# A decoder layer on one core: low weight parts of the down projections formed by an accumulating DMA

## The chip, the core and the metric

The kernel runs on one core of a Trainium2 chip. The core has five engines with a queue each: TensorE (PE, with its weight loads shown as PEld), VectorE (DVE), ScalarE (ACT), GpSimd (POOL) and SyncE (SP), and 16 DMA engines that all queues share. Each queue works in order; the queues wait for each other by semaphores. The metric is the device time of one execution in microseconds (us), lower is better; a measurement here is the median of several executions.

## What is computed

One layer over 512 tokens of 1024 channels: a gated feed-forward block (FFN), a mixing stage (a gated linear recurrence beside a convolution), and a second FFN, each followed by a layer norm. The two FFNs are what the change touches:

```python
def swiglu(x, w_gate, w_up, w_down):
    return (jax.nn.silu(x @ w_gate) * (x @ w_up)) @ w_down

x = layer_norm(ALPHA * x + 0.5 * swiglu(x, ffn1_w_gate[l], ffn1_w_up[l], ffn1_w_down[l]), ...)
...
x = layer_norm(ALPHA * x + 0.5 * swiglu(x, ffn2_w_gate[l], ffn2_w_up[l], ffn2_w_down[l]), ...)
```

`w_gate` and `w_up` are 1024 x 2816, `w_down` is 2816 x 1024, all float32.

## The kernel before

**Products from two parts.** Every float32 operand is split into a high part `hi` (the value rounded to the type that TensorE multiplies, float32r) and a low part `lo` = value - `hi`, also float32r. Each product is three matmuls, hi x hi, hi x lo and lo x hi (`mm3`, lines 185 to 187, or line 400 for the gate and up products).

**Weights.** They are split on the fly. A *unit* is a 128 x 1024 tile of weights, 512 KB. `fetch` (line 80) loads it into one of two `raw` buffers by a DMA on SP's queue, ACT rounds it into `whi` (`cast`, line 66), and DVE, or for some weights POOL, subtracts `wlo` = `raw` - `whi` (`rest`, line 69). There are six pairs of `whi` and `wlo`; `ahead(n)` fetches units in the order of the list `todo` until n are ready or in the making, so up to four units beyond the one in use. The gate and up weights come as *quads* (1 MB in one `raw` buffer, which DVE also combines into sums); a quad takes three of the six pairs.

**A gate and up step.** For each pair f of 128-column blocks (0 to 10) and for s = 0 (gate) and s = 1 (up), seven products p1 to p7 run in the order p1, p7, p2, p4, p5, p6, p3 (a Strassen-like scheme that takes seven products where eight are usual). They accumulate in two PSUM tiles `a` and `b`, and some areas are used twice, with a copy by ACT (line 420) between:

```python
                ps = {"p1": a[:, 0], "p2": a[:, 0], "p6": a[:, 1],
                      "p7": b[:, 0], "p4": b[:, 0], "p5": b[:, 1], "p3": b[:, 1]}[n]
                yield from product(ps, x, w, n, n in ("p1", "p5", "p6", "p7"))
                if n in ("p1", "p7", "p5"):
                    nc.scalar.copy(work[:, {"p1": 0, "p7": 1, "p5": 2}[n]], ps)
```

p1, for example, must have been copied before p2 goes on accumulating in the same area, and only p7 lies between them. At the end of s = 0 the gate is put through SiLU by ACT (lines 484 and 485); the result `h[f]` is finished at the end of s = 1.

**The down projection.** `rows_out` multiplies h by `w_down` in two halves of 512 output columns, 11 units each, 22 units per FFN. A unit is used by 24 matmuls of 512 columns: four token tiles, two rows of 128, three matmuls. h itself is split into `hh`, `hl` (f = 0) and `hp` (f = 1 to 10) by ACT and DVE. In the second half the last four units are kept, and the token tiles are finished one after another, each followed by its layer norm (DVE, and `rstd` on POOL). The first units of the down projection are fetched while the last gate and up step runs; units are called u0 to u21 here.

**Who sets the order.** PE's order of work in these stages is as written (`manual_schedule`); on the other engines a scheduler orders instructions by its own estimates, within the dependences. A queue then runs in that order, whatever is ready.

Of the kernel before, what the change touches and what calls it, by code (L numbers as in the profile page):

```python
# [12 lines left out]
AF = mybir.ActivationFunctionType  # L13
ALU = mybir.AluOpType
# [9 lines left out]
NP = NF // 2  # L24
# [27 lines left out]
def decoder_layer(ctx, tc, x_tok, x_q, vec, bcast, ng, w_gu1, w_d1, w_i, w_g, w_col, w_o, w_gu2, w_d2, out):  # L52
    nc = tc.nc
# [11 lines left out]
    def cast(hi, raw):  # L65
        nc.scalar.copy(hi, raw)  # L66

    def rest(lo, raw, hi, engine=nc.vector):
        engine.tensor_tensor(lo, raw, hi.bitcast(F32), op=ALU.subtract)  # L69

    def split(raw, hi, lo, lo_engine):
        cast(hi, raw)
        rest(lo, raw, hi, lo_engine)
# [3 lines left out]
    def pair_of_parts():  # L77
        return (parts.tile([P, 1024], F32R, tag="whi", name="whi"), parts.tile([P, 1024], F32R, tag="wlo", name="wlo"))

    def fetch(src, shape, lo_engine):  # L80
        raw = raws.tile([P, 1024], F32, tag="raw", name="raw")
        hi, lo = pair_of_parts()
        nc.sync.dma_start(out=raw, in_=src)
        split(raw, hi, lo, lo_engine)
        a, b = shape
        return hi.rearrange("p (a b) -> p a b", a=a), lo.rearrange("p (a b) -> p a b", a=a)

# [58 lines left out]
    def ahead(n):  # L146

        while todo and sum(r[0] for r in ready) < n:
            what, *args = todo.popleft()
            if what == "unit":  # L150
                ready.append([1, fetch(*args)])
            else:
                q = Quad(*args)
                q.load(0, 4)
                getattr(q, what)()
                ready.append([3 if what == "seven" else 2, q.of])

    def plan(srcs, shape, lo_engine):
        todo.extend(("unit", s, shape, lo_engine) for s in srcs)

    def plan_quads(src, first):
        todo.extend(("plain" if f < PLAIN else "seven", src[f, s]) for f in range(first, NP) for s in range(2))
# [7 lines left out]

    tok, ch = (2, 512), (NK, P)
    plan_quads(w_gu1, 1)
    plan([w_d1[h, u] for h in range(2) for u in range(NP)], tok, nc.vector)
    plan([w_col[n] for n in (8, 9, 10, 11)], ch, nc.vector)
    plan([w_col[n] for n in (0, 4, 1, 5, 12, 13, 14, 15)], ch, nc.gpsimd)
    plan([w_i[u] for u in range(4)], tok, nc.gpsimd)
# [2 lines left out]
    plan([w_o[0, u] for u in (2, 3)], tok, nc.gpsimd)  # L179
    plan([w_o[0, u] for u in (0, 1)] + [w_o[1, u] for u in (2, 3, 0, 1)], tok, nc.vector)  # L180
    plan_quads(w_gu2, 0)
    plan([w_d2[h, u] for h in range(2) for u in range(NP)], tok, nc.vector)

    def mm3(ps, lh, ll, rh, rl, first, last):
        nc.tensor.matmul(ps, lhsT=lh, rhs=rh, start=first, stop=False)  # L185
# [375 lines left out]
    with tc.tile_pool(name="first", bufs=1) as fst:  # L561
# [9 lines left out]
        for half, a, b in ((0, 0, 1), (0, 1, 2), (0, 2, 4), (1, 0, 2), (1, 2, 4)):  # L571
            raw = x1.raw[half][:, a:b]
# [414 lines left out]
```

## Time and profile before

| | |
|---|---|
| median of 3 runs | 954.01 us (952.9 to 954.87) |
| the profiled execution | 953.89 us, of which the span from the first to the last instruction is 952.2 us |
| PE busy | 932.9 us, 98% of the span |
| DVE, ACT, POOL busy | 699.0, 380.0, 121.7 us |
| first FFN, gate and up | about 7 to 235 us |
| first FFN, down | about 235 to 345 us |
| mixing stage | about 345 to 604 us |
| second FFN, gate and up, then down | about 604 to 824 us, 824 to 944 us |

The span is what the trace covers; the 1.7 us beside it lie outside the first and last instruction. An engine's busy time says what it did, not what it held up: that is read from the waits.

### The profile page before, as it was taken

How to read it: one execution, taken by the hardware profiler on the slowest of the kernel's cores; microseconds unless marked ns; L12 is line 12 of the kernel's file. 1: busy time of each engine (PE TensorE's matmuls, PEld its weight loads, DVE VectorE, ACT ScalarE, POOL GpSimd, SP SyncE). 2: the span in 40 equal slices, each digit the busy share in tenths (PEclk: the TensorE clock that was granted, in tenths of full speed). 3: DMA queues.
4: the chain of work that ended last, by engine and by line, in shares of the span. 5: the costliest groups of instructions: out<-in, count | busy, mean ns of one | idle time of the engine just before them, and what ended most of it. 6: DMA issues, size and time to landing. Idle time of an engine off the chain costs nothing.

```text
span 952.2 us, 14214 instructions
## 1 busy us (share of the span) xinstructions
PE 932.9 (98%) x5904; PEld 844.3 (89%) x5904; DVE 699.0 (73%) x923; ACT 380.0 (40%) x545; POOL 121.7 (13%) x107
## 2 busy tenths in 40 slices
PE   7999999999999999999999999999999999999996
PEld 6899999999888889887888878989999999988885
DVE  7978888887724275999897657958888888742417
ACT  5555555555421123313331723535555555722100
POOL 9100000000000035522352103200000000000002
PEclk9999999999999999999999999999999999999998
DMA  8432332324422303412130141222323322452202
GB/s 279 180 119 89 106 116 89 129 72 144 146 98 89 110 23 114 130 46 64 51 122 8 52 170 45 89 89 96 127 90 116 107 89 80 130 167 89 92 20 88
DMA packets 23200, 96.67 MB, mean 102 GB/s; under 512 B 2448, under 2 KB 5008, under 8 KB 17760
## 3 DMA queue, kind: packets, MB, share of 16 engines
q1 hardware_dynamic: 23024, 95.43, 29.7%
q8 instruction: 46, 0.75, 0.3%
q0 software_dynamic: 112, 0.34, 0.1%
q14 instruction: 18, 0.15, 0.1%
HBM read 93.66 MB, written 2.10 MB: 101 GB/s over the span
## 4 chain that ended last, share of the span: by engine, by line
PE 81%; DVE 10%; issue 3%; POOL 2%; DMA 1%; ACT 1%; POOLq 0%; DVEq 0%; ACTq 0%
PE bank L400 38%; PE bank L186 13%; PE bank L187 13%; PE bank L185 13%; DVE bank L745 4%; PE bank L762 2%; POOL wlo L69 1%; DMA raw<-w_col 1%; DVE wlo L69 1%; DVE m L794 1%; POOL rstd L213 1%; DVE fq L712 1%; DVE diag L802 1%; DVE xres L338 0%; DVE totals L798 0%
## 5 line engine op out<-in xcount | busy, mean ns | idle before, releaser
L69 DVE TENSOR_TENSOR wlo<-raw,whi 128x1024 fp32r<-128x1024 f32 (+2 forms) x148 | 176.9, 1201 | 147.8 <-ACT whi L66 147.7
L66 ACT CAST whi<-raw 128x1024 fp32r<-128x1024 f32 (+2 forms) x170 | 173.0, 1022 | 261.0 <-PE bank L187 149.7
L185 PE MATMUL bank<-whi,hp 128*128 128x512 f32 x320 | 124.7, 390 | 0.0
L187 PE MATMUL bank<-whi,hp 128*128 128x512 f32 x320 | 124.5, 389 | 0.0
L186 PE MATMUL bank<-wlo,hp 128*128 128x512 f32 x320 | 124.5, 389 | 0.0
L400 PE MATMUL bank<-bh,whi 128*128 128x256 f32 x432 | 122.3, 283 | 0.0
L400 PE MATMUL bank<-bl,whi 128*128 128x256 f32 x432 | 122.3, 283 | 0.0
L400 PE MATMUL bank<-ah,whi 128*128 128x256 f32 x432 | 122.2, 283 | 0.0
L400 PE MATMUL bank<-ah,wlo 128*128 128x256 f32 x432 | 122.2, 283 | 0.0
L400 PE MATMUL bank<-al,whi 128*128 128x256 f32 x432 | 122.2, 283 | 0.0
L400 PE MATMUL bank<-bh,wlo 128*128 128x256 f32 x432 | 122.1, 283 | 0.0
L400 PEld LDWEIGHTS bank<-bh,whi 128*128 128x128 f32 x432 | 82.9, 192 | 0.0
L400 PEld LDWEIGHTS bank<-bl,whi 128*128 128x128 f32 x432 | 82.9, 192 | 0.0
L400 PEld LDWEIGHTS bank<-bh,wlo 128*128 128x128 f32 x432 | 82.9, 192 | 0.0
L400 PEld LDWEIGHTS bank<-al,whi 128*128 128x128 f32 x432 | 82.8, 192 | 0.1
L400 PEld LDWEIGHTS bank<-ah,whi 128*128 128x128 f32 x432 | 82.8, 192 | 0.1
L400 PEld LDWEIGHTS bank<-ah,wlo 128*128 128x128 f32 x432 | 82.8, 192 | 0.0
L745 DVE SCALAR_TENSOR_TENSOR bank<-u,vecs,bank 128x512 f32<-128x512 f32 x120 | 82.1, 747 | 0.2
L212 POOL TENSOR_SCALAR rstd<-mv 128x1 f32<-128x1 f32 x16 | 8.1, 506 | 501.1 <-DVE mv L330 485.9
L187 PEld LDWEIGHTS bank<-whi,hp 128*128 128x128 f32 x320 | 60.1, 188 | 12.6
L185 PEld LDWEIGHTS bank<-whi,hp 128*128 128x128 f32 x320 | 60.1, 188 | 12.4
L186 PEld LDWEIGHTS bank<-wlo,hp 128*128 128x128 f32 x320 | 60.1, 188 | 12.2
(191 smaller groups left out, 1950.8 us busy)
## 6 DMA issues: line engine op xcount, KB each, us to landing
raw<-w_gu SPq DMA_DIRECT2D x42, 1024.0 KB, 4.8
raw<-w_d SPq DMA_DIRECT2D x44, 512.0 KB, 3.5
raw<-w_col SPq DMA_DIRECT2D x16, 512.0 KB, 3.5
raw<-w_o SPq DMA_DIRECT2D x8, 512.0 KB, 3.6
xres<-x_tok SPq DMA_DIRECT2D x4, 512.0 KB, 7.8
gb<-bcast SPq DMA_DIRECT2D x4, 512.0 KB, 4.3
raw<-w_i SPq DMA_DIRECT2D x4, 512.0 KB, 3.5
raw<-w_g SPq DMA_DIRECT2D x4, 512.0 KB, 3.5
```

Of the source, the lines that this page charges most:

```text
L66: nc.scalar.copy(hi, raw)
L69: engine.tensor_tensor(lo, raw, hi.bitcast(F32), op=ALU.subtract)
L185: nc.tensor.matmul(ps, lhsT=lh, rhs=rh, start=first, stop=False)
L186: nc.tensor.matmul(ps, lhsT=lh, rhs=rl, start=False, stop=False)
L187: nc.tensor.matmul(ps, lhsT=ll, rhs=rh, start=False, stop=last)
L213: nc.gpsimd.tensor_tensor(r, r, negh.broadcast_to([P, n]) if n > 1 else negh, op=ALU.pow)
L400: nc.tensor.matmul(ps, lhsT=l[:, k, :], rhs=r[:, k, :], start=first and k == 0 and j == 0, stop=k == 3 and j == 2, skip_group_check=True)
L712: nc.vector.tensor_scalar(f, s, oml[:, h:h + 1], lb[:, h:h + 1], op0=ALU.mult, op1=ALU.add)
L745: nc.vector.scalar_tensor_tensor(accs[n], us[n][:, j:j + T], vecs[:, w:w + 1], accs[n], op0=ALU.mult, op1=ALU.add)
L762: nc.tensor.matmul(ps[:, g, :], lhsT=k[:, h, sl], rhs=q[:, h, sl], start=True, stop=True)
L794: nc.vector.tensor_tensor(ov, ov, tv, op=ALU.mult)
L802: nc.vector.copy_predicated(diag[h], masks[:, n:n + 1, :].broadcast_to([P, NT, P]), ps)
```

## The change

For the 44 units of the two down projections DVE no longer subtracts. ACT makes two passes over `raw`: it rounds it into `whi` as before, and writes -`raw`, rounded to the same type, into `wlo`, which is -`whi`. Then a DMA on POOL's queue reads the same weights from memory a second time and adds them to `wlo`, so that `wlo` ends as `raw` - `whi`. A DMA that adds to its destination is issued on POOL's queue.

```diff
         nc.sync.dma_start(out=raw, in_=src)
-        split(raw, hi, lo, lo_engine)
+        if lo_engine is None:
+
+            cast(hi, raw)
+            nc.scalar.activation(lo, raw, AF.Copy, scale=-1.0)
+            nc.gpsimd.dma_start(out=lo, in_=src, accum_op=ALU.add)
+        else:
+            split(raw, hi, lo, lo_engine)
...
-    plan([w_d1[h, u] for h in range(2) for u in range(NP)], tok, nc.vector)
+    plan([w_d1[h, u] for h in range(2) for u in range(NP)], tok, None)
...
-    plan([w_d2[h, u] for h in range(2) for u in range(NP)], tok, nc.vector)
+    plan([w_d2[h, u] for h in range(2) for u in range(NP)], tok, None)
```

Lines behind the change move by six: lines 420, 484 and 485 are 426, 490 and 491 afterwards. The negation is line 87, the accumulating DMA line 88.

The change also moves instructions on the queues. On ACT, at the last gate and up pair (f = 10) of either FFN, the queue before reads as follows, from the copies of p1 and p7 of s = 0 (into `h`) over the casts of u0, u1 and u2 to the SiLU and the copy of p1 of s = 1 (into `work`):

```order
L420 COPY h<-bank_2370 128x256
L420 COPY h<-bank_2371 128x256
L66 CAST whi<-raw 128x1024 x2
L420 COPY h<-bank_2371 128x256
L66 CAST whi<-raw 128x1024
L484 ACTIVATE h<-bank_2370 128x256
L485 ACTIVATE h<-h 128x768
L420 COPY work<-bank_2484 128x256
L66 CAST hh<-h 128x1024
L420 COPY work<-bank_2485 128x256
```

And the same place of ACT's queue after the change:

```order
L426 COPY h<-bank_2370 128x256
L426 COPY h<-bank_2371 128x256
L66 CAST whi<-raw 128x1024
L87 ACTIVATE wlo<-raw 128x1024
L66 CAST whi<-raw 128x1024
L426 COPY h<-bank_2371 128x256
L87 ACTIVATE wlo<-raw 128x1024
L66 CAST whi<-raw 128x1024
L87 ACTIVATE wlo<-raw 128x1024
L490 ACTIVATE h<-bank_2370 128x256
L491 ACTIVATE h<-h 128x768
L426 COPY work<-bank_2487 128x256
```

The negation of u0 stands right behind its cast, that of u1 behind the copy of p5, and that of u2 between its cast and the SiLU, so ahead of the copy of p1 as well.

On POOL, from the scaling of the residual early in the first FFN to the first norm, the queue before holds only the clearing of two mixing buffers (`diag`) and one load (`ngb`):

```order
L288 TENSOR_SCALAR xres_76<-xres_76 128x1024
L667 MEMSET diag_3641 128x512
L665 DMA ngb<-ng 128x512
L667 MEMSET diag_3642 128x512
L212 TENSOR_SCALAR rstd<-mv 128x1
```

After the change the 22 accumulating DMAs of the first FFN stand there too:

```order
L294 TENSOR_SCALAR xres_76<-xres_76 128x1024
L88 DMA wlo<-w_d 128x1024 x2
L671 DMA ngb<-ng 128x512
L88 DMA wlo<-w_d 128x1024
L673 MEMSET diag_3663 128x512
L88 DMA wlo<-w_d 128x1024 x2
L673 MEMSET diag_3664 128x512
L88 DMA wlo<-w_d 128x1024 x17
L218 TENSOR_SCALAR rstd<-mv 128x1
```

The first five are interleaved with the load and the two clearings, and all 22 stand ahead of the norms; in the second FFN the other 22 stand in one piece ahead of the norms. PE's order is the same before and after.

## Rows read from the trace of the kernel before

**Rows 1.** Page, busy time of each engine, share, instructions.

```profile
PE 932.9 (98%) x5904; PEld 844.3 (89%) x5904; DVE 699.0 (73%) x923; ACT 380.0 (40%) x545; POOL 121.7 (13%) x107
```

**Rows 2.** Windows: us, busy by engine (instructions), granted clock, DMA share, GB/s.

```profile
52.00:235.80 183.80, 183.80 (x1516) 182.66 (x1515) 155.29 (x209) 96.78 (x145) 1.34 (x3) 1.00 0.31 105
235.80:300.00 64.20, 64.20 (x285) 53.16 (x284) 32.38 (x34) 20.41 (x21) 0.25 (x1) 1.00 0.36 116
...
824.00:890.00 66.00, 66.00 (x294) 54.71 (x293) 33.04 (x36) 21.30 (x22) 0.00 (x0) 1.00 0.36 117
```

**Rows 3.** Waits of PE, longest first: total us, times, longest.

```profile
PE bank L185 <- ACT whi L66: 5.1, 1, 5.1
PE bank L279 <- DVE xres L338: 1.2, 1, 1.2
```

**Rows 4.** Groups by line and shape: busy us, mean ns, idle before.

```profile
L69 DVE TENSOR_TENSOR wlo<-raw,whi 128x1024 fp32r<-128x1024 f32 x138 | 169.6, 1233 | 147.8 <-ACT whi L66 147.7
L66 ACT CAST whi<-raw 128x1024 fp32r<-128x1024 f32 x160 | 168.0, 1053 | 260.2 <-PE bank L187 149.7 <-PE bank L186 38.4 <-PE bank L400 30.9
```

**Rows 5.** Timeline of ACT, first FFN: start, duration, instruction, idle before.

```profile
219.45 1.05 ACT L66 CAST whi<-raw 128x1024 fp32r<-128x1024 f32 x1 [0.94 <-PE bank L400]
...
225.40 1.05 ACT L66 CAST whi<-raw 128x1024 fp32r<-128x1024 f32 x1 [1.75 <-PE bank L400]
226.59 0.39 ACT L484 ACTIVATE h<-bank 128x256 f32<-128x256 f32 x1
226.87 0.84 ACT L485 ACTIVATE h<-h 128x768 f32<-128x768 f32 x1
227.61 0.36 ACT L420 COPY work<-bank 128x256 f32<-128x256 f32 x1
```

**Rows 6.** Timelines of DVE and SP at the same place.

```profile
220.53 1.23 DVE L69 TENSOR_TENSOR wlo<-raw,whi 128x1024 fp32r<-128x1024 f32 x1 [1.45 <-ACT whi L66]
...
225.87 0.69 DVE L431 TENSOR_TENSOR h<-bank,h 128x512 f32<-128x512 f32 x1
...
221.78 0.33 SPq L83 DMA_DIRECT2D raw<-w_d  x1
```

**Rows 7.** Timeline of PE at the start of p2.

```profile
227.99 0.28 PE L400 MATMUL bank<-bh,wlo 128*128 128x256 f32 x1
228.11 0.30 PE L400 MATMUL bank<-ah,whi 128*128 128x256 f32 x1
```

**Rows 8.** Timelines of ACT and PE, the same place of the second FFN.

```profile
814.19 1.05 ACT L66 CAST whi<-raw 128x1024 fp32r<-128x1024 f32 x1 [1.69 <-DMA raw<-w_d]
815.45 0.39 ACT L484 ACTIVATE h<-bank 128x256 f32<-128x256 f32 x1 [0.21 <-DVE h L431]
...
816.46 0.36 ACT L420 COPY work<-bank 128x256 f32<-128x256 f32 x1
...
816.96 0.30 PE L400 MATMUL bank<-ah,whi 128*128 128x256 f32 x1
```

**Rows 9.** Timelines of ACT and PE in the first down projection.

```profile
251.96 1.06 ACT L66 CAST whi<-raw 128x1024 fp32r<-128x1024 f32 x1 [2.48 <-PE bank L187]
...
322.68 1.05 ACT L66 CAST whi<-raw 128x1024 fp32r<-128x1024 f32 x1 [4.38 <-PE bank L187]
...
235.65 0.40 PE L186 MATMUL bank<-wlo,hh 128*128 128x512 f32 x1
...
337.67 0.39 PE L186 MATMUL bank<-wlo,hp 128*128 128x512 f32 x1
```

**Rows 10.** Page, DMA issues: instructions, KB each, us from issue to landing.

```profile
raw<-w_gu SPq DMA_DIRECT2D x42, 1024.0 KB, 4.8
raw<-w_d SPq DMA_DIRECT2D x44, 512.0 KB, 3.5
...
xres<-x_tok SPq DMA_DIRECT2D x4, 512.0 KB, 7.8
```

**Rows 11.** Windows: four units of the down projection's steady part.

```profile
262.84:284.60 21.76, 21.76 (x97) 18.02 (x96) 4.90 (x4) 4.22 (x4) 0.00 (x0) 1.00 0.30 97
```

**Rows 12.** Timeline of POOL before the down projection.

```profile
225.80 0.60 POOL L665 DMA_DIRECT2D ngb<-ng  x1
235.52 0.53 POOL L667 MEMSET diag<- 128x512 f32 x1 [9.12 <-PE bank L400]
```

## The prediction

> **What bounds the kernel now.** I read the busy times first, then the windows by stage, then PE's waits, and last the timelines at the place where the waits nearly touch. PE is busy for 932.9 of 952.2 us [rows 1]. That is an average; the windows say where the rest lies. From 52 us to the end of the first down projection, and in the second down projection, PE's busy time equals the window: 183.80 of 183.80, 64.20 of 64.20, 66.00 of 66.00, at full granted clock [rows 2]. The list of PE's waits holds nothing of a down projection: the longest is 5.1 us in the first products of the program, the next 1.2 us at a norm [rows 3]. So in the stages that the change touches, PE alone sets the time, and there is no wait that a faster VectorE could end. What is to be found out is whether the new way of making `wlo` is late somewhere.
>
> **What is removed: nothing on the path.** 44 subtractions by DVE of 1.233 us [rows 4] are 54.3 us. PE never stood waiting for them, so they are worth 0. DVE's later work in the mixing stage is not reached by it, since the order changes only around the down projections. I find no gain to book.
>
> **What is added, in the steady part: hidden.** Each unit gets a second ACT pass, which I price like the cast beside it, 1.05 us [rows 4]; the widest other ACT row, 0.84 us for 768 columns [rows 5], would scale to 1.12 us. Back to back a pass takes about 0.1 us less (226.87 to 227.61 is 0.74 us for an instruction of 0.84 us [rows 5]), so 0.95 us. Then comes a DMA on POOL's queue. The casts of u8 and u21 are 70.72 us apart, 13 steps of 5.44 us [rows 9]; that is PE's time for a unit, and ACT sits idle for 4.38 us of each. ACT's queue has room. The tightest units are the ends. u0 is cast at 219.45 and negated by 221.45, and its `wlo` is first used at 235.65: 14.2 us are left for the DMA [rows 5, 9]. u21 is cast at 322.68, negated by 324.7, used at 337.67: 13.0 us [rows 9]. The trace has no accumulating transfer. From below it is at least a plain load of the same bytes, 3.5 us to landing; from above the slowest 512 KB of the trace, the loads of `xres`, took 7.8 us; I take 4.8 us, the row for 1024 KB, since 512 KB of weights and 512 KB of `wlo` are read [rows 10]. Either end is below 13.0 us. Without that cover every us beyond it would be a us of PE.
>
> POOL's queue is in order: a DMA that waits for its negation holds up what stands behind it. That is the `ngb` load, the two clearings of `diag` (both wanted only in the mixing stage) and, behind u21's DMA, the norms, which begin after 337.67 us, when POOL is long free. The other way round, the second clearing waits for PE until 235.52 [rows 12] and stands ahead of u5's DMA; u5 is used at 235.65 + 5 x 5.44 = 262.9, so that costs nothing.
>
> **What is added at the end of gate and up: a stall in either FFN.** Here ACT is not free to be late. In the step f = 10, s = 1, ACT must copy p1 out of PSUM before p2 accumulates there. Before the change it copies from 227.61 to 227.97 and PE starts p2 at 228.11, 0.12 us after the matmul before it, its normal pitch [rows 5, 7]. So PE waits for nothing, and has at most 0.1 us to spare (0.05 taken). Ahead of this copy in ACT's queue stand SiLU (two instructions) and u2's cast; now u2's negation comes between the cast and SiLU. Step by step, in us:
> - `raw` of u2 uses the buffer of u0. SP issues it at 221.78, as DVE's subtraction of u0 ends at 221.76 [rows 6]; the cast of u2 follows at 225.40 [rows 5]. Now the buffer comes free with u0's negation, at 219.45 + 0.95 + 1.05 = 221.45, so 0.31 earlier. But the accumulating DMA of u0 is released by that same negation and shares the DMA engines with the load. Call what this costs the load c.
> - u2: cast at 225.09 + c, negation at 226.04 + c, SiLU at 226.99 + c. SiLU was at 226.59, held by DVE's step that ended at 226.56 [rows 5, 6]. It and the copy of p1 come 0.40 + c later, and p2 0.35 + c.
> - In the second FFN the cast is at 814.19, SiLU 1.26 later and p2 at 816.96, 0.14 behind the copy's end [rows 8]: -0.31 + c + 1.90 - 1.26 = 0.33 + c, less the 0.05 to spare 0.28 + c.
>
> The two stalls sum to 0.63 + 2c. PE has no idle time behind them to take it back: all later work starts that much later.
>
> **c.** From below 0: the load may have moved its bytes before the other begins. From above 7.8 - 3.5 = 4.3 [rows 10]. A load that shares with another 512 KB should behave like one of 1024 KB, 4.8 - 3.5 = 1.3; POOL takes 0.60 to issue where SP takes 0.33 [rows 6, 12], so the other starts some 0.3 later: I take c = 1.0. Sum: 0.63 + 2.0 = 2.6 us on the profiled execution's 953.89, which is 0.12 below the median: 956.5 us, 0.3% slower. The bounds of c give 954.5 and 963.1.
>
> That row stands for a single queue, the two transfers here are on two. The Trainium skill (DMA: Bandwidth & Descriptors, Issuing engines are not separate DMA queues) says that DMAs from SP, ACT and GpSimd run on the same 16 engines and interleave. By that rule c is the whole 1.3 and the sum 3.2 us; with queues that did not touch each other it would be 0.6 us. No row here has two queues at work at once, so the trace neither bears it out nor speaks against it.
>
> **Rivals.**
> - *No measurable change.* c is small, because POOL's DMA starts to move bytes when the load has nearly landed. The deciding point is 0.63 + 2c = 1.9 us, so c = 0.64. For it: POOL's later start. Against: both are released at the same moment, and the load then has 3.5 us to go. At c = 0.1 the time is 954.7 us. 0.2%, 1.9 us, is about what a measurement of this kernel can tell from no change.
> - *The accumulating DMA is the bound.* In the steady part four plain loads keep all DMA engines busy for 0.30 of 21.76 us [rows 11], 1.63 us each. Between u0's negation at 221.45 and u21's use at 337.67 lie 116.2 us, in which 22 accumulating transfers, 20 loads and two gain and bias loads must fit: 22a + 36 = 116 gives a = 3.65, so 2.2 times a plain load. At two loads' worth (3.26) it fits. At three (4.9) each stage ends 27.7 us late: 1009 us. If they ran one after another at 7.8 us, 22 x 7.8 - 116.2 = 55.4 us per stage: 1065 us. For it: nothing in the trace bounds a transfer that adds. Against: the reads are only doubled. The Trainium skill (Collectives: The Full Stack, The bandwidth ceiling) says that a reduction is half as fast as a copy because of its second source read and not because of the add; by that rule a is 3.26 and this rival costs nothing. No run here shows it.
> - *Faster.* DVE, relieved of its `wlo` work, finishes the last sums of the gate earlier (SiLU waited for it [rows 8]) and ACT gains what the negation costs. That takes a negation behind the copy, which the queue's order rules out: the most it could give is the 0.2 us of that wait in either FFN, 953.5 us.
>
> **How the numbers follow.** The stall of 1.9 to 9 us in all: 0.56. No measurable change: 0.26. DMA as the bound: 0.14, all slower. Faster by over 0.2%: 0.04, kept for a mechanism that I do not see. So slower is 0.70, same 0.26, faster 0.04. The range leaves out the third case and the fourth: from 953.6, just under c = 0, to 962.0, c near 4.
>
> **What would show it.** PE's waits should get a new row, line 406 for ACT's copy at line 426, twice, some 1 to 2 us each, just ahead of the down projections, and on ACT's timeline u2's cast, negation, SiLU and copy should stand in one chain without idle time. The load of u2's `raw` should land 4 to 5 us after its issue. The windows of the down projections should stay full of PE. Wrong would be: waits of PE at line 192 for a DMA of `wlo` (then the second rival), or no new wait at all with c near 0 (the first). DMA share in the steady part should rise from 0.30 to 0.6 to 0.9.

## The result: 0.97% slower, by waits at the end of gate and up that the prediction had only half of

The changed kernel takes 962.22 us (961.7 to 965.97, 4 runs) where the kernel before takes 953.45 us in the same comparison (952.81 to 954.87, 4 runs): a ratio of 1.0097, 95% interval 1.0082 to 1.0113. The forecast was 956.5 us, with a range up to 962.0. The profiled execution is the slowest of the four, 965.97 us with a span of 964.3; the parts below are of its own 12.1 us of span over the one before, not of the median's 8.8.

The page's busy times and queues, to be set beside [rows 1]:

```profile
PE 938.3 (97%) x5904; PEld 848.4 (88%) x5904; DVE 646.2 (67%) x879; ACT 420.6 (44%) x589; POOL 161.7 (17%) x151
...
q1 hardware_dynamic: 23024, 95.43, 29.3%
q0 software_dynamic: 6448, 23.41, 14.2%
...
raw<-w_d SPq DMA_DIRECT2D x44, 512.0 KB, 6.6
wlo<-w_d POOLq DMA_DIRECT2D x44, 512.0 KB, 7.3
```

The change did what it says. DVE's busy time fell by 52.8 us, ACT's rose by 40.6 us, and POOL's queue (q0, the software one) moved 23.41 MB. The loads of the down projection's weights, untouched by the diff, now take 6.6 us to land where they took 3.5 [rows 10].

PE's waits, longest first; the first row has no counterpart in [rows 3]:

```profile
PE bank L406 <- ACT work L426: 6.9, 4, 2.9
PE bank L191 <- ACT whi L66: 5.0, 1, 5.0
```

There are four such waits, two in either FFN; in the same list no wait at line 192 is for a DMA, and that is where `wlo` is used. The windows say where the time goes (us, then busy time and instructions of PE, PEld, DVE, ACT, POOL, then granted clock, DMA share, GB/s):

```profile
52.00:222.00 170.00, 170.00 (x1403) 169.00 (x1402) 145.37 (x195) 88.44 (x133) 0.00 (x0) 1.00 0.29 100
222.00:232.00 10.00, 9.37 (x77) 9.12 (x77) 3.10 (x5) 6.77 (x10) 3.76 (x5) 1.00 0.93 220
232.00:236.00 4.00, 3.22 (x27) 3.02 (x26) 0.00 (x0) 2.00 (x2) 0.53 (x1) 1.00 1.04 275
236.00:242.00 6.00, 4.12 (x16) 3.83 (x17) 2.58 (x6) 4.37 (x6) 1.69 (x3) 0.60 0.98 225
242.00:248.00 6.00, 6.00 (x24) 4.85 (x23) 6.00 (x6) 4.78 (x6) 0.85 (x1) 0.84 0.95 217
...
262.00:346.00 84.00, 84.00 (x372) 69.57 (x371) 8.04 (x11) 28.07 (x28) 11.02 (x13) 1.00 0.86 200
```

Up to 222 us and from 262 us PE is as full as before. In between it idles, and its granted clock falls to 0.60 and 0.84 over two windows. The DMA engines are busy all through the change's part, already at 0.93 in the ten us in which gate and up still runs.

How a wait comes about is seen on ACT's timeline at that place (start, duration, instruction, idle before and what ended it), the counterpart of [rows 5]:

```profile
225.88 1.05 ACT L66 CAST whi<-raw 128x1024 fp32r<-128x1024 f32 x1 [0.97 <-DMA raw<-w_d]
226.84 1.05 ACT L87 ACTIVATE wlo<-raw 128x1024 fp32r<-128x1024 f32 x1
227.79 0.36 ACT L490 ACTIVATE h<-bank 128x256 f32<-128x256 f32 x1
228.06 0.83 ACT L491 ACTIVATE h<-h 128x768 f32<-128x768 f32 x1
228.79 0.36 ACT L426 COPY work<-bank 128x256 f32<-128x256 f32 x1
...
233.17 1.05 ACT L66 CAST whi<-raw 128x1024 fp32r<-128x1024 f32 x1 [2.80 <-DMA raw<-w_d]
234.12 1.05 ACT L87 ACTIVATE wlo<-raw 128x1024 fp32r<-128x1024 f32 x1
236.51 1.04 ACT L66 CAST whi<-raw 128x1024 fp32r<-128x1024 f32 x1 [1.33 <-DMA raw<-w_d]
237.46 0.36 ACT L426 COPY work<-bank 128x256 f32<-128x256 f32 x1
```

And PE's timeline, the last product before and the first after either wait, then the first down products:

```profile
228.30 0.28 PE L406 MATMUL bank<-bh,wlo 128*128 128x256 f32 x1
229.20 0.39 PE L406 MATMUL bank<-ah,whi 128*128 128x256 f32 x1 [0.63 <-ACT work L426]
...
234.94 0.28 PE L406 MATMUL bank<-bh,wlo 128*128 128x256 f32 x1
237.88 0.58 PE L406 MATMUL bank<-ah,w2hi 128*128 128x256 f32 x1 [2.65 <-ACT work L426]
238.26 0.41 PE L406 MATMUL bank<-al,w2hi 128*128 128x256 f32 x1
238.47 0.41 PE L406 MATMUL bank<-ah,w2lo 128*128 128x256 f32 x1
...
241.03 0.63 PE L192 MATMUL bank<-wlo,hh 128*128 128x512 f32 x1
241.46 0.63 PE L193 MATMUL bank<-whi,hl 128*128 128x512 f32 x1
```

First read the copy at 228.79: u2's cast, negation, SiLU and this copy stand in one chain without idle time, and p2 starts right behind it, as forecast. Then read the copy at 237.46. It is that of p5, which must be out of PSUM before p3; it stands behind u4's cast, and that cast waited until 236.5 for its load. SP issued this load at 227.9:

```profile
227.91 0.33 SPq L83 DMA_DIRECT2D raw<-w_d  x1
```

So a load that takes 3.5 us when alone [rows 10] took 8.5 us. On the chain of work that ended last it is the longest single step of that stretch:

```profile
227.91 8.52 DMA raw<-w_d
```

In the kernel before, p5's copy stood behind u4's cast too, and the cast was on time:

```profile
232.51 1.05 ACT L66 CAST whi<-raw 128x1024 fp32r<-128x1024 f32 x1 [1.83 <-PE bank L400]
233.47 0.37 ACT L420 COPY work<-bank 128x256 f32<-128x256 f32 x1
...
233.89 0.38 PE L400 MATMUL bank<-ah,w2hi 128*128 128x256 f32 x1
```

That copy ended at 233.84 and p3 began right behind it, at 233.89, so there was no room behind the cast. Ahead of it there was some: u4's load landed 1.0 us before the cast, which PE held up. Of the 4.7 us by which the load takes longer now (8.5 against 3.8 at this place before), this 1.0 us and the 0.8 us by which PE itself is late since p2 are covered; PE waits for about the rest.

The loss of the profiled execution, from matmul to matmul with the normal pitch of 0.12 us taken off, is 0.78 us at p2 and 2.82 us at p3 in the first FFN, and by the same reading 0.90 and 3.04 us in the second, 7.5 us of waiting. The last of these waits, between the matmuls before and after it:

```profile
829.94 0.28 PE L406 MATMUL bank<-bh,wlo 128*128 128x256 f32 x1
833.10 0.39 PE L406 MATMUL bank<-ah,w2hi 128*128 128x256 f32 x1 [2.88 <-ACT work L426]
```

After the waits at p3 matmuls come at about half pace, in the first FFN at once, in the second after ten matmuls at full pace (1.3 us): 0.21 us apart where 0.12 is usual, and 0.43 where 0.23 is usual for 512 columns. That is the lower of the clock's two levels, 1.2 GHz instead of 2.4 (granted clock 0.50 from 238.3 to 243.5 us). It lasts for 12 matmuls of p3 and about 8 of the longer ones in the first FFN (12 x 0.094 + 8 x 0.2 = 2.7 us) and about 8 of the longer ones in the second (1.6 us). Together with the waits that is 11.8 of the 12.1 us.

The clock's part differs from execution to execution. The mean granted clock was 0.993 here and 0.996, 0.996 and 0.998 in the other three, where the executions of the kernel before have 0.995 to 0.999. The one at 0.998 took 962.60 us, so a loss of some 9 us arises also where the clock shows no loss. How much of the median's 8.8 us the clock makes stays open, as only the slowest of the four was profiled.

### The profile page after: what moved, and what is told of

It is laid out like the page before. It is cut to its first block, busy times and chain, and to the rows that moved or that the text cites. A ratio compares the mean times of both kernels' runs of the same rounds, so it can differ in the third digit from the quotient of the medians.

```text
span 964.3 us, 14287 instructions
## 1 busy us (share of the span) xinstructions
PE 938.3 (97%) x5904; PEld 848.4 (88%) x5904; DVE 646.2 (67%) x879; ACT 420.6 (44%) x589; POOL 161.7 (17%) x151
## 3 DMA queue, kind: packets, MB, share of 16 engines
q0 software_dynamic: 6448, 23.41, 14.2%
## 4 chain that ended last, share of the span: by engine, by line
PE 77%; DVE 11%; issue 4%; DMA 3%; ACT 2%; POOL 2%; POOLq 0%; DVEq 0%; ACTq 0%
PE bank L406 35%; PE bank L192 13%; PE bank L193 13%; PE bank L191 13%; DVE bank L751 4%; DMA raw<-w_d 3%; PE bank L768 2%; DVE xres L344 1%; POOL wlo L69 1%; DVE wlo L69 1%; ACT whi L66 1%; DVE m L800 1%; POOL rstd L219 1%; DVE fq L718 1%; DVE diag L808 1%
## 5 line engine op out<-in xcount | busy, mean ns | idle before, releaser
L69 DVE TENSOR_TENSOR wlo<-raw,whi 128x1024 fp32r<-128x1024 f32 (+2 forms) x104 | 123.2, 1193 | 66.9 <-ACT whi L66 66.9
L88 POOL DMA_DIRECT2D wlo<-w_d x44 | 38.0, 863 | 572.1 <-ACT wlo L87 551.0
L330 DVE SCALAR_TENSOR_TENSOR xres<-bank,xres 128x512 f32<-128x512 f32 x24 | 16.4, 687 | 131.3 <-PE bank L193 131.3
L87 ACT ACTIVATE wlo<-raw 128x1024 fp32r<-128x1024 f32 x44 | 46.6, 1059 | 93.6 <-PE bank L192 68.7
L193 PEld LDWEIGHTS bank<-whi,hp 128*128 128x128 f32 x320 | 60.1, 188 | 12.6
```

What stands on the lines that cost most here:

```text
L87: nc.scalar.activation(lo, raw, AF.Copy, scale=-1.0)
L88: nc.gpsimd.dma_start(out=lo, in_=src, accum_op=ALU.add)
L193: nc.tensor.matmul(ps, lhsT=ll, rhs=rh, start=False, stop=last)
L330: nc.vector.scalar_tensor_tensor(z, acc[i], factor, z, op0=ALU.mult, op1=ALU.add)
```

## The experiments

Two theories were set against each other, and a third beside them. **Late loads**: the accumulating DMAs crowd the loads of u2 to u4; the casts of these units wait in ACT's queue ahead of the copies of p1 and p5, and PE waits for the copies. **A longer ACT queue**: the second passes delay the copies by themselves. **Steady traffic**: DMA engines nine tenths full cost PE time all through the down projection. In all these kernels only the lines shown differ from the changed kernel.

**First five units back to DVE.**

```diff
-    plan([w_d1[h, u] for h in range(2) for u in range(NP)], tok, None)
+    plan([w_d1[0, u] for u in range(5)], tok, nc.vector)
+    plan([w_d1[h, u] for h in range(2) for u in range(NP) if h or u >= 5], tok, None)
...
```

(and the same for `w_d2`, here and below).

> The first five units of each down projection go back to VectorE; the other 17 keep the negation and the accumulating DMA. Theory of late loads (accumulating DMAs crowd the raw loads of u2 to u4, the casts of these wait in ACT's queue ahead of the copies of p1 and p5, PE waits): nothing is late while gate and up still runs, so 953.5 us, within 1.9 us of before. Theory of a longer ACT queue (the extra passes alone delay the copies): the passes of u0 to u4 are gone too, so also 953.5. Theory of steady traffic (DMA engines nearly full through the down projection cost PE time or clock there): 17 of 22 units still load them, so about 960.

954.15 us, ratio 1.0006 (0.9996 to 1.0015): no difference from before. Its windows in the first down projection:

```profile
222.00:236.00 14.00, 14.00 (x112) 13.71 (x112) 9.56 (x14) 9.70 (x14) 1.61 (x3) 1.00 0.58 175
...
250.00:262.00 12.00, 12.00 (x55) 9.94 (x54) 0.00 (x0) 3.99 (x4) 1.72 (x2) 1.00 1.02 269
262.00:346.00 84.00, 84.00 (x377) 69.66 (x376) 14.22 (x21) 26.35 (x27) 12.40 (x15) 1.00 0.77 174
```

The DMA engines are nearly as busy (up to 1.02, and 0.77 over the stretch in which the change has 0.86), and PE is full at full clock. Steady traffic is out.

**Only the first five units by DMA.** The same split with `None` and `nc.vector` exchanged.

> The reverse: only the first five units of each down projection are formed by the negation and the accumulating DMA, the other 17 by VectorE. Late loads: the whole loss stays, 960 to 964 us, with PE's waits for ACT's copies at the end of gate and up. Longer ACT queue: the same, 960 to 964. Steady traffic: only 5 of 22 units, about 955.

967.16 us, ratio 1.0131 (1.0099 to 1.0163): five units of 22 carry the whole loss. PE's waits in this run are the same four:

```profile
PE bank L408 <- ACT work L428: 7.8, 4, 3.9
```

Its median is above the full change's, which was not expected; the two intervals overlap, and the profiled executions took 966.4 and 966.0 us, so that it is slower is not shown. Its longest wait is 3.9 us where the change's is 2.9: in the second FFN u4's load landed after 9.8 us, in the change after 8.7. Why is not known.

**The same queue, a sixteenth of the traffic.**

```diff
-            nc.gpsimd.dma_start(out=lo, in_=src, accum_op=ALU.add)
+            nc.gpsimd.dma_start(out=lo[:, 0:64], in_=src[:, 0:64], accum_op=ALU.add)
```

> As the change, with the same order on ACT, but the accumulating DMA covers only the first 64 of the 1024 columns, a sixteenth of the bytes (the other columns of the low parts stay at minus the high part, so the outputs are not the layer's). Late loads: the loads of u2 to u4 are nearly as quick as before the change, the wait at p5 goes and only the 0.4 us or so at p1 in either FFN stay: 954 to 955 us. Longer ACT queue: nothing gained, 960 to 964. Steady traffic: 953.5 to 955.

954.56 us, ratio 1.0002 (0.9988 to 1.0017). ACT's timeline, in the order of the change:

```profile
225.08 1.05 ACT L66 CAST whi<-raw 128x1024 fp32r<-128x1024 f32 x1 [0.48 <-DMA raw<-w_d]
226.04 1.05 ACT L87 ACTIVATE wlo<-raw 128x1024 fp32r<-128x1024 f32 x1
226.99 0.36 ACT L490 ACTIVATE h<-bank 128x256 f32<-128x256 f32 x1
227.26 0.84 ACT L491 ACTIVATE h<-h 128x768 f32<-128x768 f32 x1
227.99 0.36 ACT L426 COPY work<-bank 128x256 f32<-128x256 f32 x1
...
232.90 1.05 ACT L66 CAST whi<-raw 128x1024 fp32r<-128x1024 f32 x1 [0.87 <-PE bank L406]
233.85 0.37 ACT L426 COPY work<-bank 128x256 f32<-128x256 f32 x1
```

Here the prediction's chain stands with c = 0: the cast at 225.08 (225.09 forecast), SiLU at 226.99, the copy of p1 0.38 us later than before, and p2 0.30 us later (0.35 forecast). And u4's cast no longer waits for a load but for PE, as in the kernel before. All the extra passes are there, and no difference from before is left that the measurement can tell.

**ACT's queue as before, the traffic kept.**

```diff
-            nc.scalar.activation(lo, raw, AF.Copy, scale=-1.0)
+            nc.gpsimd.tensor_scalar(lo, raw, -1.0, 1.0, op0=ALU.mult, op1=ALU.mult)
```

> As the change, but POOL makes the negation, so that ACT's queue reads as before the change; the accumulating DMAs and their traffic stay. Late loads: the casts of u2 and u4 still wait for their loads ahead of ACT's copies, so the wait at p5 stays, 958 to 964 us. Longer ACT queue: 953.5. Steady traffic: 960 to 964.

962.49 us, ratio 1.0092 (1.0075 to 1.0109), as slow as the change. ACT's timeline, with the order of before:

```profile
231.63 1.05 ACT L66 CAST whi<-raw 128x1024 fp32r<-128x1024 f32 x1 [2.57 <-DMA raw<-w_d]
235.37 1.04 ACT L66 CAST whi<-raw 128x1024 fp32r<-128x1024 f32 x1 [2.69 <-DMA raw<-w_d]
236.32 0.36 ACT L426 COPY work<-bank 128x256 f32<-128x256 f32 x1
```

The waits at p1 are gone and those at p5 are there (2.40 and 2.52 us). Together with the run before this settles it between the two theories: the traffic without ACT's second passes costs the time, the passes with a sixteenth of the traffic do not.

**No DMA, DVE adds.**

```diff
-            nc.gpsimd.dma_start(out=lo, in_=src, accum_op=ALU.add)
+            nc.vector.tensor_tensor(lo, lo.bitcast(F32), raw, op=ALU.add)
```

> As the change, with ACT's second pass for every unit, but VectorE adds the weights to the negated high part from the raw buffer, so there is no accumulating DMA and no second read of the weights. Late loads: raw loads land after 3.5 us as before, no wait at p5; at most some 0.4 us at p1 in either FFN: 953.5 to 955 us. A longer ACT queue by itself: 960 or more. Clock: without a wait of 2 us or more the granted clock stays at 1.00 in the down projections.

958.51 us, ratio 1.0053 (1.0037 to 1.0069): a miss for both theories, since late loads had 953.5 to 955 and a longer queue 960 or more. ACT's timeline shows why:

```profile
226.53 1.05 ACT L66 CAST whi<-raw 128x1024 fp32r<-128x1024 f32 x1 [1.74 <-DMA raw<-w_d]
227.49 0.37 ACT L490 ACTIVATE h<-bank 128x256 f32<-128x256 f32 x1
227.76 0.83 ACT L491 ACTIVATE h<-h 128x768 f32<-128x768 f32 x1
228.50 1.04 ACT L87 ACTIVATE wlo<-raw 128x1024 fp32r<-128x1024 f32 x1
229.44 0.64 ACT L426 COPY work<-bank 128x256 f32<-128x256 f32 x2
```

The add needs both the negation and `raw`, so u0's buffer comes free only after cast, negation and add, about 1.0 us later after u0's cast than before; u2's load starts late with no DMA of POOL's beside it, and its negation still stands ahead of p1's copy. PE waits 1.41 and 1.40 us at p2, and 0.26 us once at p3. That is 3.1 us of the timed 5.1; the profiled execution, the fastest of its four, shows no more. The granted clock stays at 1.00 over these waits. So lateness of u2's load is paid at p1 without an accumulating DMA too: about 1.0 of the 1.4 us is the late load, and the rest, about what the passes alone cost in the run with a sixteenth of the traffic (0.30), goes with the negation. "The passes cost next to nothing" holds only while u2's load is on time.

**A plain DMA in place of the accumulating one.**

```diff
-            nc.gpsimd.dma_start(out=lo, in_=src, accum_op=ALU.add)
+            nc.gpsimd.dma_start(out=lo, in_=src)
```

> As the change, but POOL's DMA overwrites the low part with the weights instead of adding to it: the same bytes from memory and the same writes, without the second read and the add (the low parts are then the weights themselves, so the outputs are not the layer's). If it is the add that makes the transfer heavy, the DMA takes about 1.6 us of all engines in place of about 3.1, the loads of u3 and u4 land in about 5 us in place of 8, and PE waits for the copy of p5 for less than 1 us: 954 to 957 us. If any second 512 KB transfer beside the loads does it, 960 to 964.

955.74 us, ratio 1.0025 (1.0016 to 1.0035): three quarters of the loss is gone. The page's DMA lines:

```profile
q0 software_dynamic: 6448, 23.41, 7.9%
...
raw<-w_d SPq DMA_DIRECT2D x44, 512.0 KB, 4.4
wlo<-w_d POOLq DMA_DIRECT2D x44, 512.0 KB, 3.9
```

The same bytes counted, but 7.9% of 953.5 us over 44 transfers is 1.7 us of all engines each, where the accumulating queue's 14.2% of 964.3 us is 3.1. PE waits 0.71 us at p3 of the first FFN instead of 2.65, and not at all at p3 of the second. It is that the transfer accumulates, more than a second transfer as such, that makes the loads late. What in the accumulating weighs, a second read or the addition itself, no run here separates.

**The second FFN alone.** Only `w_d2` with `None`.

> The change in the second FFN's down projection alone. Late loads, with a loss of its own at the end of either gate and up: half of the whole loss, 956 to 960 us, with PE's two waits for ACT's copies only before the second down projection. If the loss of the first FFN were what counts (for example because the mixing stage is entered late), 953.5.

959.85 us, ratio 1.0067 (1.005 to 1.0084): the second FFN pays on its own, 6.4 us where the whole change costs 8.8. The first alone was not run. The waits, 0.35 and 2.99 us, stand before the second down projection, and the granted clock falls behind them, to a mean of 0.83 from 828 to 838 us.

**First three units back to DVE.** As the first experiment with 3 in place of 5.

> Only the first three units of each down projection go back to VectorE; u3 and u4, whose casts stand ahead of the copy of p5, keep the negation and the accumulating DMA. Late loads: the transfers of u0 to u2 are what crowds the loads of u3 and u4; without them the casts are on time although ACT's queue holds the passes of u3 and u4: 953 to 955 us. If the accumulating DMAs of u3 and u4 or their passes matter, 957 or more.

954.14 us, ratio 1.0004 (0.9992 to 1.0016). u3 and u4 keep both passes and their accumulating DMAs, and nothing is lost that can be told: PE has no wait at p2 and a single one at p3, of 0.3 us in the second FFN. It is the transfers of u0 to u2, at work while u3 and u4 are loaded, that do the harm. (The passes of u0 to u2 are gone here too; that they are not the cause rests on the run with a sixteenth of the traffic.) None of the versions beats the kernel before, which had no wait of PE here to remove.

## Why the prediction failed, step by step

- **What bounds the kernel**: right. PE alone; taking the subtractions from DVE brought nothing, as the versions with three and five units on DVE show (1.0004 and 1.0006 with DVE relieved of 38 and 34 subtractions).
- **Hidden in the steady part**: right, with less room than the 4.8 us that were taken for a landing. An accumulating transfer landed after 5.5 to 10.4 us (median 7.3), within the 13.0 us that the tightest unit has, and the DMA share of 0.86 is within the 0.6 to 0.9 that was named. Its load on the DMA engines is 3.1 us by the queue's share, 1.9 plain loads on SP's queue (1.8 plain transfers on POOL's), against 3.26 taken and 3.65 as the breaking point. The second rival is out by these numbers. The rule of the Trainium skill that was cited for it (Collectives: The Full Stack, The bandwidth ceiling), half speed because of the second source read, agrees with the 1.9; its reason is not tested by a run here.
- **The stall at p1**: right in place and mechanism, and right in size once c is put in. u2's load landed after 4.0 us in the first FFN and 4.1 in the second, its cast came at 225.88; with the first FFN running 0.30 us later there from the start that makes c = 0.49, and 0.35 + 0.49 = 0.84 us compares with 0.78 measured. In the second FFN c = 0.66 and 0.28 + 0.66 = 0.94 compares with 0.90. c was taken as 1.0, so the two waits that were forecast came to 1.7 us, less than the 2.6. The rule of the Trainium skill (DMA: Bandwidth & Descriptors, Issuing engines are not separate DMA queues) agrees with the trace in that loads land later beside POOL's transfers (8.5 us for u4's). At u2 c was not the whole 1.3 us: the load was issued at 221.78, and POOL was still issuing u0's transfer until 223.0.
- **"The two stalls sum to 0.63 + 2c"**: this is the step that failed. It stopped at the first copy, and put the second at nothing without a reason. The copy of p5 behind u4's cast, later in the same step, has no more room: before the change it followed that cast at once, and p3 followed the copy. The loads of u3 and u4 meet not one accumulating DMA at its start but those of u0, u1 and u2, which are under way at the same time, and u4's is late not by 1.0 but by some 5 us (8.5 and 8.7 instead of 3.5). That is the 5.9 us of waiting at p3 in the two FFNs. c was priced at one load and used as if it were the loads' only lateness.
- **The clock**: not in the sum at all. The waits at p3 were followed by stretches at the lower level that cost another 4.3 us in the profiled execution, and less in the others by their mean clocks. PE's time had been taken as fixed.
- **The rivals**: "no measurable change" hung on c at u2 below 0.64. c came out below and near it (0.49 and 0.66), and the time still rose, since the rival counted the same two waits. The measured 962.22 us lies close to the upper end of the range, and a loss of 8.8 us within the "1.9 to 9" of the case that was called likeliest; but in that sum it would take a c near 4, and c was about 0.5, so this nearness is chance. The range also ended at 962.0 although its own bound of c gave 963.1.

What stays open: how much of the median's loss the clock makes, why loads come later still in the version with only five units by DMA, and what the 2 us of the DVE-adds version beyond its shown waits are.

## What to carry to other kernels

Before a transfer is added beside others, list every instruction that waits for one of the others and what stands behind it in its queue; the price can be paid at each of them, and here most of it was paid at the second. Where a busy engine is fed through a short in-order queue, its slack at the tightest hand-over counts (here under 0.1 us), not the idle share of the queue's engine (ACT was 60% idle). Work taken from an engine that nobody waited for was worth nothing, and a wait in a matmul-bound stretch can cost more than its length (2.8 us of waiting and 2.7 us at the lower clock behind it, in the first FFN of the profiled execution).

## What was not expected of the hardware

An accumulating DMA of 512 KB from memory into on-chip memory kept the 16 DMA engines busy for 3.1 us, against 1.7 us for the plain transfer on the same queue, and loads on the other queue landed after 6.6 us (median) beside it, 4.4 us beside the plain one and 3.5 us alone. And TensorE's granted clock fell to the lower level after it had stood idle for 2.4 to 3.9 us in a stretch otherwise full but for one shorter wait at most, at each of the seven waits of that length in the profiled executions of the change and the runs above. It stayed at 1.00 over the waits of 1.4 us where DVE adds, and over one of 2.0 us at the norm behind the first FFN where POOL negates.
